# Gated linear attention: scores and query-state products as plain fp32 matmuls instead of three split ones

## The chip, the cores and the metric

The kernel runs on one core of one Trainium2 chip. The metric is the device time of one execution in microseconds (us). The engines are PE (the matrix engine; its weight loads are listed on their own as PEld), DVE (VectorE, elementwise work), ACT (ScalarE, activations and copies), POOL (GpSimd, nearly unused here) and SP (SyncE, which issues the DMAs).

## The reference

One layer of an encoder block on 1024 tokens of width 1024, all in float32: a projection, a gated linear attention that runs in both directions, a windowed attention, gates that merge the two, an output projection and a gated feed-forward part. What matters here is the linear attention (4 heads, keys of 128, values of 256):

```python
def _gla_direction(q, k, v, log_g, include_diag):
    ...
    b = jnp.cumsum(log_g, axis=3)
    b_last = b[:, :, :, -1:, :]
    q_dec = q * jnp.exp(b)
    k_inv = k * jnp.exp(-b)
    k_tail = k * jnp.exp(b_last - b)
    mask = jnp.tril(jnp.ones((c, c), dtype=bool), k=0 if include_diag else -1)
    scores = jnp.where(mask, jnp.einsum("bhncd,bhnmd->bhncm", q_dec, k_inv), 0.0)
    o_intra = jnp.einsum("bhncm,bhnme->bhnce", scores, v)
    chunk_kv = jnp.einsum("bhnmd,bhnme->nbhde", k_tail, v)
    ...
    o_inter = jnp.einsum("bhncd,nbhde->bhnce", q_dec, states)
    return (o_intra + o_inter).reshape(bsz, nh, s, dv)
```

It is called once forward and once on the flipped sequence; the two outputs are added. Two of the products are touched by the change: `scores` (decayed queries with inversely decayed keys) and `o_inter` (decayed queries with the running state).

## The kernel before, in words

Nearly all matrix products are made in "split" form: a float32 operand x is cut into a high part h (a copy rounded to the type fp32r, made by ACT) and a low part l = x - h (made by DVE, also fp32r), and the product is three fp32r matmuls, h·h + h·l + l·h, added up in PSUM. This is `mm3` (line 78); `mm` (line 75) is a single matmul, whose form follows the type of its operands. A few matmuls are plain fp32: the warm-up (line 384) and the sums over squares (lines 417, 421, 1010).

The linear attention is one stage. Head by head, the 1024 tokens are cut into chunks of 128 (c = 0 to 7), two chunks make a pair. Five functions do the work of a chunk:

- `g_gates` (line 481, once a pair): loads queries and keys into `qk`, computes the gates and their running sums (`e`, `cs`), and from them the decayed keys of both directions `en` and the decayed queries. Lines 529 and 530 write the queries over `cs` (forward) and `e` (backward); lines 531 to 538 split keys into `kh`, `kl` and queries into `q2f` (forward) and `q2b` (backward), high part in slot 0, low part in slot 1.
- `g_scores` (line 540): splits the values (`vh`, `vl`), transposes the keys and splits them (`kth`, `ktl`), makes the scores of both directions with `mm3` (lines 558 to 560), merges them through a mask into `sp` and splits that (`sh`, `sl`).
- `g_out` (line 569): the chunk's key-value products, the forward state `pf`, the decayed forward state split into `th`, `tl` (lines 581 to 584), and the output: scores times values, plus queries times state (line 594).
- `g_back` and `g_back_out` (lines 598 and 613): the backward state `kb`, its decayed form split into `thb`, `tlb`, and the product of backward queries with it (line 617).
- `g_turn` (line 633): the transposed output, stored to DRAM.

The order of PE is written out by hand (`manual_schedule`, line 660). Step t of lines 662 to 664 runs what the table `at` holds for it: the gates of a pair first, then the transposes of finished chunks, the backward product, `g_out`, and `g_scores`. Scores of chunk n come two steps after step n, its output three steps after. Between them `fill` inserts a fixed number of dense matmuls (46, then 26, then 24 a step) of projections that other stages need. The order of the other engines is not in the source: a planner places their instructions by readiness and modelled cost, and each engine then runs its list strictly in order. A tile with `bufs=2` is one of two buffers; a new tile waits until every reader of the buffer's last owner is done. `q2f` has two buffers, `q2b` of a pair one to three, `cs` and `e` one.

Of the kernel before, what the change touches and what calls it, by code (L numbers as in the profile page):

```python
# [30 lines left out]
def body(tc, i, out):  # L31
    nc = tc.nc
    with ExitStack() as root:
# [447 lines left out]
        def g_gates(hd, c):  # L481


            pr = Chunk()
            for j in range(2):
                a = gla[hd, c + j] = Chunk()
                a.pr, a.j, a.t = pr, j, slice(j * P, (j + 1) * P)
            s, co = c // 4, (c % 4) * P
            for nme in ("q", "k"):
                need((f"{nme}{hd}", s))  # L490
            qk = gtile("qk", (P, 2, 256))
            nc.sync.dma_start(out=qk[:, 0], in_=scr[f"q{hd}", s][:, co:co + 256])
            nc.sync.dma_start(out=qk[:, 1], in_=scr[f"k{hd}", s][:, co:co + 256])
            if hd == 0:

                r = rstd[:, c * P:(c + 2) * P]
                nc.vector.scalar_tensor_tensor(qk[:, 0], qk[:, 0], 128 ** -0.5, r, op0=ALU.mult, op1=ALU.mult)
                nc.vector.tensor_tensor(qk[:, 1], qk[:, 1], r, op=ALU.mult)
            z = chtile((P, 2, 256))
            for d in range(2):  # L500
                mm(z[:, d], upS[:, d, hd * P:(hd + 1) * P], lrS[:, c * P:(c + 2) * P], True, True)
            e = gtile("e", (P, 2, 2, P), bufs=1)
            ef = e.rearrange("p d j t -> p (d j t)")
            nc.scalar.activation(ef, z.rearrange("p d t -> p (d t)"), AF.Exp, scale=-1.0)

            nc.vector.tensor_scalar(ef, ef, float(np.expm1(8.0)), None, op0=ALU.min)
            nc.scalar.activation(ef, ef, AF.Ln, bias=ones[:, 0:1])

            cs = gtile("cs", (P, 2, 2, P), bufs=1)
            csf = cs.rearrange("p d j t -> p (d j t)")  # L510
            nc.vector.tensor_tensor_scan(csf, mask.rearrange("p c t -> p (c t)"), ef, 0.0, op0=ALU.mult, op1=ALU.add)

            pr.sm = gtile("sm", (P, 2, 2, 2), bufs=16)
            nc.vector.tensor_scalar(pr.sm, cs[:, :, :, 63:128:64], -1.0 / 16, None, op0=ALU.mult)
            nc.vector.tensor_tensor(pr.sm[:, :, :, 1], pr.sm[:, :, :, 1], pr.sm[:, :, :, 0], op=ALU.subtract)

            nc.vector.tensor_tensor(e[:, 0], cs[:, 0], cs[:, 0, :, 63:64].to_broadcast([P, 2, P]), op=ALU.subtract)
            nc.vector.tensor_tensor(e[:, 1, :, 1:P], cs[:, 1, :, 0:P - 1], cs[:, 1, :, 63:64].to_broadcast([P, 2, P - 1]),
                                    op=ALU.subtract)
            nc.vector.tensor_scalar(e[:, 1, :, 0:1], cs[:, 1, :, 63:64], -1.0, None, op0=ALU.mult)  # L520

            x1 = cs.rearrange("p d j t -> p d (j t)")
            x2 = e.rearrange("p d j t -> p d (j t)")
            nc.scalar.activation(csf, ef, AF.Exp, scale=-1.0 / 16)
            nc.scalar.activation(ef, ef, AF.Exp, scale=1.0 / 16)
            pr.en = gtile("en", (P, 2, 256))
            nc.vector.tensor_tensor(pr.en[:, 0], x2[:, 0], qk[:, 1], op=ALU.mult)
            nc.vector.tensor_tensor(pr.en[:, 1], x1[:, 1], qk[:, 1], op=ALU.mult)
            nc.vector.tensor_tensor(x1[:, 0], x1[:, 0], qk[:, 0], op=ALU.mult)
            nc.vector.tensor_tensor(x2[:, 1], x2[:, 1], qk[:, 0], op=ALU.mult)  # L530
            pr.kh = gtile("kh", (P, 2, 256), FR)
            pr.kl = gtile("kl", (P, 2, 256), FR)
            nc.scalar.activation(pr.kh, pr.en, AF.Copy)
            nc.vector.tensor_tensor(pr.kl, pr.en, pr.kh.bitcast(F32), op=ALU.subtract)
            pr.q2 = (gtile("q2f", (P, 2, 256), FR), gtile(f"q2b{c}", (P, 2, 256), FR, bufs=(3, 2, 2, 1)[c // 2]))
            for q2, x in zip(pr.q2, (x1[:, 0], x2[:, 1])):
                nc.scalar.activation(q2[:, 0], x, AF.Copy)
                nc.vector.tensor_tensor(q2[:, 1], x, q2[:, 0].bitcast(F32), op=ALU.subtract)

        def g_scores(hd, c):  # L540

# [14 lines left out]
            nc.vector.tensor_tensor(a.ktl, kt, a.kth.bitcast(F32), op=ALU.subtract)  # L556
            sc = chtile((P, 2, P))
            for d in range(2):
                mm3(sc[:, d], a.pr.kh[:, d, a.t], a.pr.kl[:, d, a.t], a.pr.q2[d][:, 0, a.t], a.pr.q2[d][:, 1, a.t],
                    True, True)  # L560
            sp = gtile("sp", (P, P))
            nc.scalar.copy(sp, sc[:, 0])
            nc.vector.copy_predicated(sp, tri, sc[:, 1])
# [5 lines left out]
        def g_out(hd, c):  # L569
# [6 lines left out]
            if c:  # L576
                pf = gla[hd, c - 1].pf
                dec = gtile("dec", (P, 1))
                p = gla[hd, c - 1]
                nc.scalar.activation(dec, a.pr.sm[:, 0, a.j, 0:1], AF.Exp, bias=p.pr.sm[:, 0, p.j, 1:2])  # L580
                th = gtile("th", dt=FR)
                tl = gtile("tl", dt=FR)
                nc.scalar.activation(th, pf, AF.Copy, scale=dec[:, 0:1])
                nc.vector.scalar_tensor_tensor(tl, pf, dec[:, 0:1], th.bitcast(F32), op0=ALU.mult, op1=ALU.subtract)
                nc.vector.scalar_tensor_tensor(a.pf, pf, dec[:, 0:1], kv[:, 0], op0=ALU.mult, op1=ALU.add)
                a.kb = gtile(f"kb{c}", bufs=2 if c < 5 else 1)
                nc.scalar.copy(a.kb, kv[:, 1])
            else:
                nc.vector.tensor_copy(a.pf, kv[:, 0])
                a.kb = None  # L590
            o = chtile((P, 256))
            mm3(o, a.sh, a.sl, a.vh, a.vl, True, c == 0)
            if c:
                mm3(o, a.pr.q2[0][:, 0, a.t], a.pr.q2[0][:, 1, a.t], th, tl, False, True)
            a.ob = gtile(f"ob{c}", bufs=2 if c < 5 else 1)
            nc.scalar.copy(a.ob, o)

        def g_back(hd, c):

            a = gla[hd, c]  # L600
            if c < NC - 1:
                n = gla[hd, c + 1]
                dec = gtile("decb", (P, 1))
                nc.scalar.activation(dec, a.pr.sm[:, 1, a.j, 1:2], AF.Exp, bias=n.pr.sm[:, 1, n.j, 0:1])
                th = gtile("thb", dt=FR)
                tl = gtile("tlb", dt=FR)
                nc.scalar.activation(th, n.kb, AF.Copy, scale=dec[:, 0:1])
                nc.vector.scalar_tensor_tensor(tl, n.kb, dec[:, 0:1], th.bitcast(F32), op0=ALU.mult, op1=ALU.subtract)
                if c:
                    nc.vector.scalar_tensor_tensor(a.kb, n.kb, dec[:, 0:1], a.kb, op0=ALU.mult, op1=ALU.add)  # L610
                a.thb, a.tlb = th, tl

        def g_back_out(hd, c):
            a = gla[hd, c]
            if c < NC - 1:
                o2 = chtile((P, 256))
                mm3(o2, a.pr.q2[1][:, 0, a.t], a.pr.q2[1][:, 1, a.t], a.thb, a.tlb, True, True)
                nc.vector.tensor_tensor(a.ob, a.ob, o2, op=ALU.add)
            if c:
                g_back(hd, c - 1)  # L620
# [773 lines left out]
```

## Time and profile before

| what | value |
|---|---|
| three runs | 1664.22, 1664.38, 1662.86 us; median 1664.22 |
| the profiled execution's own time | its span, 1661.5 us from the first to the last instruction; no other time of it is recorded |
| granted clock of PE, mean | 1.000 |
| linear attention stage with its filling | about 196 to 545 us of the span |
| windowed attention with its filling | about 545 to 765 us |
| output projections, merge | about 765 to 1035 us |
| feed-forward, two parts | about 1035 to 1448 and 1448 to 1661 us |

A row of the profile's groups reads: line, engine, operation, tiles written and read, shapes, count, then busy us and mean ns of one, then the idle time of the engine just before them and what ended it. L76 is the single matmul inside `mm`, so the tiles tell which product it is; `ch` and `mm` are tiles in PSUM. A row of a timeline reads: start, duration, engine, line, operation, tiles; several like records that follow each other are merged, with their count.

### The profile page before, as it was taken

To read this page: it belongs to the slowest core of one execution; us is meant where nothing else is said; L and a number is where in the kernel's file an instruction comes from. 1 tells how busy PE (TensorE), PEld (TensorE's weight loads), DVE (VectorE), ACT (ScalarE), POOL (GpSimd) and SP (SyncE) were. 2 spreads that over 40 slices of the span, in tenths; PEclk is the share of its full clock that TensorE was granted. 3 is DMA by queue.
4 is the path that set the end of the run, shared out by engine and by line. 5 is a ranking of instruction groups with operands and counts; after the bars stand their busy time and mean duration, and the time that the engine had idled before them with its cause. 6 is when DMAs were issued, how large, how long until landed. Compare 5 with 4: busy or idle time off the path is not lost.

```text
span 1661.5 us, 23685 instructions
## 1 busy us (share of the span) xinstructions
PE 1648.4 (99%) x7792; PEld 1368.2 (82%) x7792; DVE 1259.9 (76%) x2616; ACT 890.7 (54%) x1880; POOL 0.2 (0%) x4
## 2 busy tenths in 40 slices
PE   9999999999999999999999999999999999999999
PEld 7888888888888878887888888888888888888887
DVE  8766766888875898866886578887778877779655
ACT  8522464687877588776644556433333333354442
POOL 0000000000000000000000000000000000000000
PEclk9999999999999999999999999999999999999999
DMA  7444452344435633228866645353234444496433
GB/s 235 144 133 145 153 166 92 110 137 125 133 115 156 203 120 105 91 72 257 254 212 190 177 143 169 108 166 117 93 101 151 165 141 133 159 344 198 148 96 120
DMA packets 157499, 252.41 MB, mean 152 GB/s; under 512 B 18142, under 2 KB 43486, under 8 KB 157376
## 3 DMA queue, kind: packets, MB, share of 16 engines
q1 hardware_dynamic: 157376, 250.90, 48.0%
q8 instruction: 61, 1.00, 0.3%
q14 instruction: 62, 0.51, 0.1%
HBM read 183.46 MB, written 67.37 MB: 151 GB/s over the span
## 4 chain that ended last, share of the span: by engine, by line
PE 87%; DVE 5%; ACT 4%; DMA 3%; issue 1%; SPq 0%; ACTq 0%; DVEq 0%
PE mm L76 33%; PE mm L306 7%; PE mm L308 7%; PE mm L307 7%; PE mm L1207 7%; PE ch L76 7%; PE ch L1207 5%; PE ch L308 3%; PE ch L306 3%; PE ch L307 3%; PE ch L830 1%; DVE wl L72 0%; DMA kvr<-skv 0%; DMA wr<-in_w_fi_dram 0%; PE ch L637 0%
## 5 line engine op out<-in xcount | busy, mean ns | idle before, releaser
L70 ACT ACTIVATE wh<-wr 128x512 fp32r<-128x512 f32 x238 | 148.3, 627 | 103.1 <-PE mm L76 77.7
L72 DVE TENSOR_TENSOR wl<-wr,wh 128x512 fp32r<-128x512 f32 x238 | 162.4, 685 | 42.7 <-ACT wh L70 42.0
L298 ACT ACTIVATE wh<-ws 128x512 fp32r<-128x512 f32 x120 | 75.7, 632 | 176.0 <-PE mm L307 84.7
L76 PE MATMUL mm<-wl,xh 128*128 128x512 f32 x320 | 127.4, 398 | 0.0
L76 PE MATMUL mm<-wh,xh 128*128 128x512 f32 x320 | 126.6, 396 | 0.8 <-DVE xc L376 0.8
L76 PE MATMUL mm<-wh,xl 128*128 128x512 f32 x320 | 126.5, 395 | 0.0
L76 PE MATMUL mm<-xh,wh 128*128 128x512 f32 x256 | 103.0, 403 | 0.2 <-ACT wh L70 0.2
L76 PE MATMUL mm<-xl,wh 128*128 128x512 f32 x256 | 102.1, 399 | 0.1
L299 DVE TENSOR_TENSOR wl<-ws,wh 128x512 fp32r<-128x512 f32 x120 | 82.0, 684 | 22.6 <-ACT wh L298 22.6
L298 ACT ACTIVATE wh<-wr 128x512 fp32r<-128x512 f32 x60 | 37.9, 632 | 105.2 <-issue 49.4
L298 ACT ACTIVATE wh<-a 128x512 fp32r<-128x512 f32 x64 | 40.5, 633 | 90.9 <-PE ch L1207 42.3
L76 PE MATMUL mm<-xh,wl 128*128 128x512 f32 x256 | 88.8, 403 | 0.0
L299 DVE TENSOR_TENSOR wl<-a,wh 128x512 fp32r<-128x512 f32 x64 | 44.2, 690 | 42.8 <-ACT wh L298 42.4
L76 PEld LDWEIGHTS mm<-wh,xh 128*128 128x128 f32 x320 | 60.2, 188 | 11.3 <-DVE xc L376 1.2
L76 PEld LDWEIGHTS mm<-wh,xl 128*128 128x128 f32 x320 | 60.2, 188 | 10.5
L76 PEld LDWEIGHTS mm<-wl,xh 128*128 128x128 f32 x320 | 60.2, 188 | 10.1
L1207 PE MATMUL mm<-hh,wh 128*128 128x512 f32 x176 | 68.5, 389 | 0.0
L1207 PE MATMUL mm<-hl,wh 128*128 128x512 f32 x176 | 68.5, 389 | 0.0
L1207 PE MATMUL mm<-hh,wl 128*128 128x512 f32 x176 | 68.5, 389 | 0.0
L1177 DVE TENSOR_TENSOR hl<-hr,hh 128x512 fp32r<-128x512 f32 x75 | 51.3, 684 | 3.8 <-ACT hh L1176 3.7
L76 PEld LDWEIGHTS mm<-xl,wh 128*128 128x128 f32 x256 | 48.2, 188 | 7.1 <-DVE xl L251 0.7
L76 PEld LDWEIGHTS mm<-xh,wh 128*128 128x128 f32 x256 | 48.2, 188 | 6.9 <-ACT wh L70 0.7
(579 smaller groups left out, 4880.8 us busy)
## 6 DMA issues: line engine op xcount, KB each, us to landing
wr<-in_w_fi_dram SPq DMA_DIRECT2D x102, 256.0 KB, 2.9
wr<-in_w_f_dram SPq DMA_DIRECT2D x80, 256.0 KB, 2.8
wr<-in_w_t_dram SPq DMA_DIRECT2D x80, 256.0 KB, 2.8
B<-c SPq DMA_DIRECT2D x44, 256.0 KB, 2.2
T<-tx SPq DMA_DIRECT2D x44, 256.0 KB, 3.0
a<-in_w_fo_dram SPq DMA_DIRECT2D x44, 256.0 KB, 5.4
hr<-T SPq DMA_DIRECT2D x44, 256.0 KB, 2.7
wr<-in_w_ob_dram SPq DMA_DIRECT2D x32, 256.0 KB, 3.1
```

Of the source, the lines that this page charges most:

```text
L70: nc.scalar.activation(h, raw, AF.Copy)
L72: nc.vector.tensor_tensor(l, raw, h.bitcast(F32), op=ALU.subtract)
L76: nc.tensor.matmul(o, a, b, start=start, stop=stop)
L298: nc.scalar.activation(h, src, AF.Copy)
L299: nc.vector.tensor_tensor(l, src, h.bitcast(F32), op=ALU.subtract)
L306: nc.tensor.matmul(o, h[:, c], x[kk][0], start=start and kk == 0, stop=False, skip_group_check=True)
L307: nc.tensor.matmul(o, h[:, c], x[kk][1], start=False, stop=False, skip_group_check=True)
L308: nc.tensor.matmul(o, l[:, c], x[kk][0], start=False, stop=kk == nk - 1, skip_group_check=True)
L830: nc.tensor.transpose(pt[:, h], a.p[:, h, (kb - a.b0) * P:(kb - a.b0 + 1) * P], ident)
L1177: nc.vector.tensor_tensor(l, r, h.bitcast(F32), op=ALU.subtract)
L1207: nc.tensor.matmul(ys[m], a[:, c], b, start=f0, stop=f1, skip_group_check=True)
```

## The change

Queries, keys and decayed states are no longer split. The decayed queries go straight into `q2f` and `q2b` as float32 (128 x 256 instead of two parts), the scores take `en` and these in one plain fp32 matmul a direction instead of three fp32r ones, and the decayed states `th` and `thb` are single float32 tiles that are multiplied with the queries in one plain fp32 matmul each. `kh`, `kl`, `tl` and `tlb` disappear with the instructions that made them. Values, transposed keys, masked scores, the key-value products and everything outside this stage stay split.

```diff
@@ g_gates
-            nc.vector.tensor_tensor(x1[:, 0], x1[:, 0], qk[:, 0], op=ALU.mult)
-            nc.vector.tensor_tensor(x2[:, 1], x2[:, 1], qk[:, 0], op=ALU.mult)
-            pr.kh = gtile("kh", (P, 2, 256), FR)
-            pr.kl = gtile("kl", (P, 2, 256), FR)
-            nc.scalar.activation(pr.kh, pr.en, AF.Copy)
-            nc.vector.tensor_tensor(pr.kl, pr.en, pr.kh.bitcast(F32), op=ALU.subtract)
-            pr.q2 = (gtile("q2f", (P, 2, 256), FR), gtile(f"q2b{c}", (P, 2, 256), FR, bufs=(3, 2, 2, 1)[c // 2]))
-            for q2, x in zip(pr.q2, (x1[:, 0], x2[:, 1])):
-                nc.scalar.activation(q2[:, 0], x, AF.Copy)
-                nc.vector.tensor_tensor(q2[:, 1], x, q2[:, 0].bitcast(F32), op=ALU.subtract)
+            pr.q2 = (gtile("q2f"), gtile(f"q2b{c}", bufs=(3, 2, 2, 1)[c // 2]))
+            nc.vector.tensor_tensor(pr.q2[0], x1[:, 0], qk[:, 0], op=ALU.mult)
+            nc.vector.tensor_tensor(pr.q2[1], x2[:, 1], qk[:, 0], op=ALU.mult)
@@ g_scores
             for d in range(2):
-                mm3(sc[:, d], a.pr.kh[:, d, a.t], a.pr.kl[:, d, a.t], a.pr.q2[d][:, 0, a.t], a.pr.q2[d][:, 1, a.t],
-                    True, True)
+                mm(sc[:, d], a.pr.en[:, d, a.t], a.pr.q2[d][:, a.t], True, True)
@@ g_out
-                th = gtile("th", dt=FR)
-                tl = gtile("tl", dt=FR)
+                th = gtile("th")
                 nc.scalar.activation(th, pf, AF.Copy, scale=dec[:, 0:1])
-                nc.vector.scalar_tensor_tensor(tl, pf, dec[:, 0:1], th.bitcast(F32), op0=ALU.mult, op1=ALU.subtract)
...
             if c:
-                mm3(o, a.pr.q2[0][:, 0, a.t], a.pr.q2[0][:, 1, a.t], th, tl, False, True)
+                mm(o, a.pr.q2[0][:, a.t], th, False, True)
@@ g_back
-                th = gtile("thb", dt=FR)
-                tl = gtile("tlb", dt=FR)
-                nc.scalar.activation(th, n.kb, AF.Copy, scale=dec[:, 0:1])
-                nc.vector.scalar_tensor_tensor(tl, n.kb, dec[:, 0:1], th.bitcast(F32), op0=ALU.mult, op1=ALU.subtract)
+                a.thb = gtile("thb")
+                nc.scalar.activation(a.thb, n.kb, AF.Copy, scale=dec[:, 0:1])
...
-                a.thb, a.tlb = th, tl
@@ g_back_out
-                mm3(o2, a.pr.q2[1][:, 0, a.t], a.pr.q2[1][:, 1, a.t], a.thb, a.tlb, True, True)
+                mm(o2, a.pr.q2[1][:, a.t], a.thb, True, True)
```

## The prediction

> **What bounds the kernel now.** I read the page first, then the stretch of the program that the change touches, then the waits of PE in it.
>
> ```profile
> span 1661.5 us, 23685 instructions
> PE 1648.4 (99%) x7792; PEld 1368.2 (82%) x7792; DVE 1259.9 (76%) x2616; ACT 890.7 (54%) x1880; POOL 0.2 (0%) x4
> PE 87%; DVE 5%; ACT 4%; DMA 3%; issue 1%; SPq 0%; ACTq 0%; DVEq 0%
> ```
>
> PE is busy 99% of the span and holds 87% of the chain that ended last. The ends of matmuls are modelled, so I do not use their durations; I use the distance from one start to the next, which is what a record costs in an unbroken stream.
>
> ```profile
> 196.00:545.00 349.00, 346.81 (x1897) 295.18 (x1898) 255.88 (x692) 244.78 (x654) 0.00 (x0) 1.00 0.44 133
> ```
>
> This is the table by stretches; the columns are the stretch, its length, then the busy time of PE, weight loads, DVE, ACT and POOL, and the granted clock. It is the linear attention stage with its dense filling. The clock is granted in full (1.00), PE is busy 346.81 of 349.00 us, DVE 255.88 and ACT 244.78. So DVE and ACT work is worth something here only where PE waits for it:
>
> ```profile
> PE ch L76 <- DVE sh L566: 1.1, 3, 0.7
> PE ch L76 <- DVE ktl L556: 0.5, 1, 0.5
> ```
>
> These are the rows of PE's waits (total us, times, longest). Only these two kinds in the stage, 1.6 us together, wait for work of linear attention. The change is therefore first a sum over matmul records, and second the end of four short waits.
>
> **The matmuls that are replaced.** Counts first:
>
> ```profile
> L76 PE MATMUL ch<-q2f,kh 128*128 128x128 f32 x64 | 13.3, 290 | 0.0
> L76 PE MATMUL ch<-q2b,kh 128*128 128x128 f32 x64 | 12.4, 276 | 0.0
> L76 PE MATMUL ch<-th,q2f 128*128 128x256 f32 x56 | 14.5, 281 | 0.0
> L76 PE MATMUL ch<-thb,q2b 128*128 128x256 f32 x56 | 14.5, 281 | 0.1
> ```
>
> In these names the moving operand stands before the stationary one. Each triple uses its high stationary (scores) or its high moving operand (states) twice, so there are 32 + 32 = 64 triples for scores (128 columns move) and 28 + 28 = 56 for products with states (256 columns move). Their rhythm, from the timeline of PE (start, us, engine, line):
>
> ```profile
> 385.57 0.42 PE L76 MATMUL ch<-q2f,kh 128*128 128x128 f32 x2
> 385.83 0.28 PE L76 MATMUL ch<-q2f,kl 128*128 128x128 f32 x1
> 385.94 0.39 PE L76 MATMUL ch<-q2b,kh 128*128 128x128 f32 x2
> 386.16 0.27 PE L76 MATMUL ch<-q2b,kl 128*128 128x128 f32 x1
> 386.27 0.45 PE L76 MATMUL mm<-xh,wh 128*128 128x512 f32 x1
> ```
>
> The six score records of one chunk take 386.27 - 385.57 = 0.70 us, 0.117 each; the first carries about 0.03 from the transposes before it, which stays, and the rest go at 0.112 (385.94 to 386.16 is two records).
>
> ```profile
> 384.15 0.28 PE L76 MATMUL ch<-th,q2f 128*128 128x256 f32 x1
> 384.27 0.28 PE L76 MATMUL ch<-tl,q2f 128*128 128x256 f32 x1
> 384.39 0.28 PE L76 MATMUL ch<-th,q2f 128*128 128x256 f32 x1
> 384.51 0.40 PE L76 MATMUL mm<-xh,wl 128*128 128x512 f32 x1
> ```
>
> A state product takes 384.51 - 384.15 = 0.36 us, 0.119 a record. So a record of 256 columns costs hardly more than one of 128.
>
> **What a plain fp32 matmul costs.** The kernel has a few already: the warm-up of line 384, the sums over squares of line 417 (512 columns) and of line 421 (2 columns).
>
> ```profile
> 4.68 0.94 PE L76 MATMUL ch<-ones 128*128 128x128 f32 x7
> 47.30 1.88 PE L76 MATMUL ch<-acc,ones 128*128 128x512 f32 x4
> 49.01 1.84 PE L76 MATMUL ch<-ones,acc 128*128 128x2 f32 x16
> ```
>
> Line 417 issues two matmuls and leaves four records, line 421 issues eight and leaves sixteen: a plain fp32 matmul is two records. With 512 columns one record takes (49.01 - 47.30) / 4 = 0.428 us. With 2 columns it takes 0.11 (1.84 us for sixteen, the last end modelled), and with 128 columns, at the end of the warm-up, (0.94 - 0.275) / 6 = 0.111, where 0.275 is about the length of one such record. So there is a floor of about 0.112 a record, for 2 columns as for 128, and above it the time grows with the columns. No row shows 256 columns in plain fp32. Without any shape assumed it lies between 0.112 and 0.428. The split matmuls say how it goes between: a 512-column record there costs 0.227,
>
> ```profile
> 1448.31 29.92 PE mm L1207 x132
> ```
>
> (29.92 / 132, from the chain of waits), and a 256-column one 0.119, or 52% of it. Plain fp32 at 256 is then between 0.214 (half of 0.428) and 0.224 (52%); I take 0.214, as at 0.214 the floor of 0.112 is far away.
>
> **The sum.** Scores: per triple three records become two, 3 x 0.112 = 0.336 to 2 x 0.112 = 0.224, 64 times: -7.2 us (with 0.117 a record before, -8.1). State products: 3 x 0.119 = 0.357 to 2 x 0.214 = 0.428, 56 times: +4.0 us (at 0.224: +5.1). PE's stream becomes 3.2 us shorter, between 2.1 and 4.2. PE's order is fixed by hand and the filling counts dense matmuls, not time, so all of this reaches the end of the stage, and from there the end.
>
> The two parts of the change pull against each other: the scores sit on the floor, where a record less is a gain, and the state products stand above it, where plain fp32 streams longer than three split records.
>
> The Trainium skill, "FP8 and Floating Point Precision", section "TensorE Precision Notes", states a rule that speaks against the change: true fp32 takes four passes through the array. The trace agrees as to streaming, since two records at 0.428 are four times half a record; it does not agree as to four loads, since it has two records a matmul. What the sum is if each of four passes pays the floor stands below as a rival.
>
> **What goes from DVE and ACT.**
>
> ```profile
> L534 DVE TENSOR_TENSOR kl<-en,kh 128x512 fp32r<-128x512 f32 x16 | 10.9, 684 | 0.1
> L538 DVE TENSOR_TENSOR q2f<-cs,q2f 128x256 fp32r<-128x256 f32 x16 | 6.7, 417 | 0.0
> L608 DVE SCALAR_TENSOR_TENSOR tlb<-kb,decb,thb 128x256 fp32r<-128x256 f32 x28 | 13.4, 480 | 4.8 <-ACT thb L607 4.4
> L533 ACT ACTIVATE kh<-en 128x512 fp32r<-128x512 f32 x16 | 9.9, 621 | 0.4 <-DVE en L527 0.4
> ```
>
> DVE loses 16 of the first, 16 of the second and as many for q2b, and 28 of the third with 28 like it in line 584: 10.9 + 2 x 6.7 + 2 x 13.4 = 51 us of busy time. ACT loses line 533 and the two copies of line 537. All of it is hidden behind PE's 346.81 us except where PE waited. The longest of those waits, DVE's and PE's timeline together:
>
> ```profile
> 248.84 0.68 DVE L534 TENSOR_TENSOR kl<-en,kh 128x512 fp32r<-128x512 f32 x1
> 249.43 0.41 DVE L538 TENSOR_TENSOR q2f<-cs,q2f 128x256 fp32r<-128x256 f32 x1
> 249.77 0.41 DVE L538 TENSOR_TENSOR q2b<-e,q2b 128x256 fp32r<-128x256 f32 x1
> ...
> 250.43 0.23 DVE L566 CAST sh<-sp 128x128 fp32r<-128x128 f32 x1
> 249.74 0.28 PE L76 MATMUL ch<-vh,ktl 128*128 128x256 f32 x1
> 250.71 0.39 PE L76 MATMUL ch<-vh,sh 128*128 128x256 f32 x1 [0.68 <-DVE sh L566]
> ```
>
> PE needs sh and gets it 0.97 us after the record before, 0.85 more than 0.12. Right in front of sh on DVE stand kl, q2f and q2b, which the change takes out: from 248.84 to about 250.10, 1.26 us, more than PE waited. So this wait ends, and by the same order the other three, which are shorter. From start to start they cost 0.85 / 0.68 times what the page counts, so 1.6 us are about 2.0 us (estimate). I take -2.0; the ends are 0, if something else on the way to sh comes next, such as the copy of the scores by ACT, and -2.0.
>
> The multiplies of lines 529 and 530 stay, 417 ns each, but write into q2f and q2b instead of over cs and e. No DMA is added, removed or moved, and the ACT copies th and thb stay, with another output type, at no change (estimate, from the like copies around).
>
> Together -3.2 - 2.0 = -5.2 us: the span goes from 1661.5 to 1656.3. The median of the runs (1664.22) stands 2.7 above the span of the profiled execution; I take this distance as constant: **1659.0 us**.
>
> One term has no row: DVE's and ACT's order is set anew by the planner when instructions go, here and in the windowed attention behind. In the order of before PE's waits in the stage are 1.6 us, and behind it the largest is
>
> ```profile
> PE ch L76 <- DVE pl L834: 1.5, 1, 1.5
> ```
>
> A new order could lose these or have as many more; I take 0, with about 3 us to each side.
>
> **The rivals.**
>
> *A. Only the matmuls count.* New waits take the place of the old ones, and -3.2 alone is left: 1661.0. For it: the four waits are accidents of one order of DVE, and the next order may have its own. Against it: DVE loses a fifth of its 255.88 us.
>
> *B. Four passes that each pay the floor.* Scores 4 x 0.112 instead of 3 x 0.112, 64 times, +7.2; states 4 x 0.119 instead of 3 x 0.119, 56 times, +6.7; with the waits gone 1664.2 + 13.9 - 2.0 = 1676. Against it: two records for each matmul in the rows above.
>
> *C. The write of q2f blocks DVE.* This is the rival on the other side. q2f has two buffers, and the product of forward states of the odd chunk two pairs back still reads the old one in the very group of steps in which the gates write the new one. Before, copies filled q2f, well after the multiply; now the multiply itself writes it:
>
> ```profile
> 384.15 0.42 DVE L529 TENSOR_TENSOR cs<-cs,qk 128x256 f32<-128x256 f32 x1
> 389.14 0.22 DVE L566 CAST sh<-sp 128x128 fp32r<-128x128 f32 x1
> 390.15 0.28 PE L76 MATMUL ch<-vh,sh 128*128 128x256 f32 x1
> ```
>
> PE reads the old q2f from 384.15 to about 384.67 (the rows of the state product), so the multiply at 384.15 would hold DVE for some 0.5 us, with en, pf, ktl and sh queued behind it. But sh has 390.15 - 389.36 = 0.8 us of slack, and about 0.6 + 0.33 + 0.33 + 0.40 = 1.7 us of DVE work ahead of it (kl, q2f, q2b, tl) goes. The block decides only from 2.5 us on. If the planner put the multiply so early that it held DVE for 3.2 us, 0.7 in each of 14 groups (16 pairs of chunks, less the first two, which find free buffers): 1664.2 - 3.2 + 9.8 = 1671.
>
> *D. More waits end.* All of PE's waits in this stage and the longest behind it: -4.2 from the matmuls, -2.0, -1.5 to -3: about 1656.
>
> **How the numbers follow.** Chances: the forecast 0.58, A 0.22, D 0.10, C 0.06, B 0.04. What one can tell from no change here is about 0.2%, 3.3 us. The forecast and D lie beyond it, A just within (3.2), B and C on the other side: faster 0.68; some of the forecast's own spread and some of A's cross the bound in both directions, which I let cancel; within 0.2% 0.22, slower 0.10. The range reaches from 1654.5 (D with the better end) to 1664.0 (A with the weaker end of the matmuls, 2.1, and a new order that costs 2 us); it leaves out B, C and a little beyond.
>
> **What would show it.** In the changed profile score records come as 128 records of "q2f,en" and "q2b,en" at 0.112 from start to start, state records as 112 with 256 columns at 0.214; rows of kl, kh, tl and tlb are gone; the waits of PE for sh and ktl at 249, 267 and 286 us are gone; the stage ends about 5 us earlier, and everything behind is shifted by as much. Records of 256 columns at 0.25 or more, four records a matmul, or a DVE multiply into q2f that waits long for PE, would prove me wrong.

## The result and the profile after

| kernel | median of the runs | lowest to highest | span of the profiled execution |
|---|---|---|---|
| before | 1664.27 us (4 runs) | 1662.86 to 1664.38 | 1661.5 us |
| after | 1657.02 us (4 runs) | 1656.48 to 1659.58 | 1655.7 us |

The ratio is 0.9951, with a 95% interval of 0.994 to 0.9962: the changed kernel is faster by half a per cent, 7.2 us, and the interval does not reach 1.

The page of the changed kernel, first its span, then the busy times, then the chain that ended last:

```profile
span 1655.7 us, 23275 instructions
PE 1643.6 (99%) x7672; PEld 1362.6 (82%) x7672; DVE 1221.1 (74%) x2512; ACT 873.3 (53%) x1832; POOL 0.2 (0%) x4
PE 90%; DVE 3%; ACT 3%; DMA 2%; issue 1%; SPq 0%; DVEq 0%; ACTq 0%
```

PE has 120 records fewer (7792 to 7672): 64 triples and 56 triples became pairs of records. DVE has lost 38.8 us of busy time and ACT 17.4. PE's share of the last chain went from 87% to 90%, DVE's from 5% to 3%.

The groups of the new matmuls (counts are records):

```profile
L76 PE MATMUL ch<-th,q2f 128*128 128x256 f32 x56 | 16.7, 380 | 0.0
...
L76 PE MATMUL ch<-q2b,en 128*128 128x128 f32 x64 | 12.4, 275 | 0.0
```

The backward state products and the forward scores have rows with the same counts. 28 state products in each direction left 56 records, 32 score matmuls left 64: two records for each plain fp32 matmul, as in the rows of the sums over squares before. Their rhythm, from the timeline of PE in the middle of the stage:

```profile
378.63 0.60 PE L76 MATMUL ch<-th,q2f 128*128 128x256 f32 x2
378.88 0.82 PE L76 MATMUL mm<-xh,wl 128*128 128x512 f32 x2
379.54 0.39 PE L76 MATMUL mm<-xh,wh 128*128 128x512 f32 x1
...
380.22 0.39 PE L76 MATMUL ch<-q2f,en 128*128 128x128 f32 x2
380.44 0.39 PE L76 MATMUL ch<-q2b,en 128*128 128x128 f32 x2
```

There is a trap in such rows. From the start of the state product to the next row are only 0.25 us, which looks like two records of 0.125. But the two 512-column records behind it then take 379.54 - 378.88 = 0.66 us instead of 2 x 0.227 = 0.45. So the start noted for the second record of a plain matmul is not to be taken at its word here: its time shows up behind the next record. Over both rows, 379.54 - 378.63 - 0.45 = 0.46 us go to this state product. So single gaps mislead, and I used sums.

That can be done exactly here. PE's order is written by hand, and the 7432 records that do not belong to the changed products follow each other in the same order in every kernel compared here. Laid side by side, each gap between two starts has a counterpart, and the differences can be summed by what lies in the gap. A gap with a changed product is taken together with the gap behind it, since part of the product's time shows up there. From 190 to 545 us of the kernel before, in us, after minus before:

| what lies in the gap | gaps | difference |
|---|---|---|
| the scores of a chunk | 32 | -7.23 |
| forward state product | 28 | +1.88 |
| backward state product | 28 | +1.84 |
| other records of 256 columns (here PE waited for sh, sl, ktl) | 292 | -3.15 |
| other records of 512 and 128 columns | 1092 | -0.40 |
| the stage | | -7.06 |

The stage by itself, in the table by stretches, and what is left of PE's waits from 190 to 560 us:

```profile
196.00:540.00 344.00, 343.50 (x1786) 291.00 (x1787) 217.14 (x588) 228.10 (x607) 0.00 (x0) 1.00 0.45 137
```

```profile
PE mm L76 <- DVE xc L376: 0.8, 1, 0.8
```

PE was idle 2.19 us of the stage before (349.00 - 346.81) and is idle 0.50 us now. The only wait listed belongs to the entry into the stage and was there before. No wait for sh or ktl is listed any more, though of the last one (287 us before) two gaps of 0.22 us instead of 0.12 remain (283.59 to 284.03). Why they ended can be seen at the place of the longest one, in the timelines of DVE and PE:

```profile
246.75 0.42 DVE L530 TENSOR_TENSOR q2f<-cs,qk 128x256 f32<-128x256 f32 x1
...
247.43 0.42 DVE L531 TENSOR_TENSOR q2b<-e,qk 128x256 f32<-128x256 f32 x1
247.76 0.42 DVE L549 TENSOR_TENSOR ktl<-ch,kth 128x256 fp32r<-128x256 f32 x1
248.09 0.29 DVE L555 COPY_PREDICATED sp<-tri,ch 128x128 f32<-128x128 uint32 x1
248.42 0.23 DVE L558 CAST sh<-sp 128x128 fp32r<-128x128 f32 x1
...
249.54 0.48 DVE L575 SCALAR_TENSOR_TENSOR pf<-pf,dec,ch 128x256 f32<-128x256 f32 x1 [0.57 <-PE ch L76]
249.22 0.28 PE L76 MATMUL ch<-vh,ktl 128*128 128x256 f32 x1
249.34 0.28 PE L76 MATMUL ch<-vh,sh 128*128 128x256 f32 x1
```

sh is done at 248.65 and read at 249.34, 0.69 us to spare, where PE had waited 0.68. Now it is DVE that waits for PE (the 0.57 before pf).

The stage begins at the same distance from the span's start as before (0.1 us later), ends 6.95 us earlier, and the last matmul of the program starts 5.8 us earlier: 1.2 us were given back behind the stage, in gaps of the windowed attention (0.46 at 755 us, 0.2 at 770) and of the later products (0.45 at 1061, 0.16 at 1459). A second profiled execution of the change, below, gives back 1.1 us, at 755 and 770 again but not at 1061. Why these gaps are longer was not followed up.

### The profile page after: what moved, and what is told of

It reads as the page before. It is cut to its first block, busy times and chain, and to the rows that moved or that the text cites. A ratio compares the mean times of both kernels' runs of the same rounds, so it can differ in the third digit from the quotient of the medians.

```text
span 1655.7 us, 23275 instructions
## 1 busy us (share of the span) xinstructions
PE 1643.6 (99%) x7672; PEld 1362.6 (82%) x7672; DVE 1221.1 (74%) x2512; ACT 873.3 (53%) x1832; POOL 0.2 (0%) x4
## 4 chain that ended last, share of the span: by engine, by line
PE 90%; DVE 3%; ACT 3%; DMA 2%; issue 1%; SPq 0%; DVEq 0%; ACTq 0%
PE mm L76 36%; PE ch L76 8%; PE mm L306 7%; PE mm L308 7%; PE mm L307 7%; PE mm L1194 7%; PE ch L1194 5%; PE ch L306 3%; PE ch L307 3%; PE ch L308 3%; PE ch L817 1%; DMA kvr<-skv 1%; DMA lo<-b 0%; PE ch L624 0%; PE ch L545 0%
## 5 line engine op out<-in xcount | busy, mean ns | idle before, releaser
L76 PE MATMUL mm<-wh,xh 128*128 128x512 f32 x320 | 130.8, 409 | 0.8 <-DVE xc L376 0.8
```

What stands on the lines that cost most here:

```text
L76: nc.tensor.matmul(o, a, b, start=start, stop=stop)
```

## The experiments

The theory at the start: PE sets the time. Each score triple that loses a record gains 0.112 us, each state product loses about 0.07, and the work that goes from DVE and ACT is worth the waits it ends and no more. The rivals: the gain comes from DVE and ACT and not from the matmuls; or it comes from a luckier order of the planner. Every ratio below is against the kernel before on the same chip.

The stage as the gaps between PE's starts show it, all against the same profiled execution of before (us):

| kernel | scores | forward states | backward states | other 256-column gaps | the rest | stage |
|---|---|---|---|---|---|---|
| change | -7.23 | +1.88 | +1.84 | -3.15 | -0.40 | -7.06 |
| change again | -7.23 | +1.87 | +1.85 | -3.14 | -0.59 | -7.24 |
| plain scores only | -7.24 | +0.64 | -0.41 | -0.92 | -0.25 | -8.18 |
| plain scores only, again | -7.23 | +0.66 | -0.36 | -0.95 | -0.33 | -8.21 |
| plain states only | +0.10 | +2.04 | +1.82 | -1.43 | -0.30 | +2.23 |
| change, all splits still made | -7.23 | +3.44 | +1.83 | +1.46 | +0.32 | -0.18 |
| change, key and query splits still made | -7.23 | +3.22 | +2.48 | +0.95 | -0.29 | -0.87 |
| change, state splits still made | -7.23 | +1.87 | +1.85 | -2.55 | +0.08 | -5.98 |
| plain scores, low parts of queries on POOL | -7.24 | +1.30 | -0.37 | -0.14 | -0.15 | -6.60 |
| before, low parts on POOL | 0.00 | +0.79 | -0.35 | +10.04 | +3.13 | +13.61 |
| plain scores, late query splits | -7.23 | -0.04 | -0.37 | -1.96 | -0.47 | -10.07 |

### Each half by itself

Plain scores only: keys are not split, queries still are, for the state products, which stay split.

```diff
-            pr.kh = gtile("kh", (P, 2, 256), FR)
-            pr.kl = gtile("kl", (P, 2, 256), FR)
...
+            pr.qs = (gtile("qsf"), gtile("qsb"))
+            nc.vector.tensor_tensor(pr.qs[0], x1[:, 0], qk[:, 0], op=ALU.mult)
+            nc.vector.tensor_tensor(pr.qs[1], x2[:, 1], qk[:, 0], op=ALU.mult)
...
-            for q2, x in zip(pr.q2, (x1[:, 0], x2[:, 1])):
+            for q2, x in zip(pr.q2, pr.qs):
...
+                mm(sc[:, d], a.pr.en[:, d, a.t], a.pr.qs[d][:, a.t], True, True)
```

> Only the scores are plain fp32; the products with states stay split (queries keep a float32 copy beside their two parts, keys are not split). The ledger theory (scores -7.2 us, state products +3.7 to +4, ended waits about -3): the state term is gone, the score term stays, and with kl gone from DVE most of the waits end: -7.2 and -1 to -3, about 1655 us, faster than the changed kernel. The rival (the forms of the matmuls cancel, the gain is the 51 us of DVE work less): only 11 us of DVE work go, so no better than about 1662.

Measured: 1655.92 us against 1665.7, ratio 0.9937 (0.9924 to 0.9949); measured again on another chip:

> The kernel with plain scores and split state products once more, beside the changed kernel. The ledger theory: PE's own records are 3.7 us shorter than in the change (no plain state products), of which the splits that it keeps on DVE give back 2 to 3 as waits: 0 to 3 us faster than the change, ratio to before 0.993 to 0.995. The rival (DVE's relief is what counts): slower than the change, since DVE keeps 40 of the 51 us.

1655.23 us against 1665.22, 0.994 (0.9928 to 0.9953). Beside it, on the same chip, ran the change itself:

> The changed kernel itself, on the same chip and against the same runs of before as the next three. Both theories: the ratio of the first comparison again, 0.994 to 0.996.

1656.14 us, 0.9947 (0.9934 to 0.9959). The scores' gain is the same -7.23 in every kernel that has plain scores. Half the change is at least as good as the whole: the medians are 0.9 us apart and the traces' stages 1.0 us, but the intervals overlap. So the rival that the gain comes from DVE's and ACT's lesser work fails: by it, with only 11 of 51 us of DVE work gone, this kernel should have stayed near 1662 us.

Plain states only: queries and keys are split for the scores as before, the states are not.

```diff
+            pr.kh = gtile("kh", (P, 2, 256), FR)
+            pr.kl = gtile("kl", (P, 2, 256), FR)
...
+            pr.qs = (gtile("qsf", (P, 2, 256), FR), gtile("qsb", (P, 2, 256), FR))
+            for qs, x in zip(pr.qs, pr.q2):
+                nc.scalar.activation(qs[:, 0], x, AF.Copy)
+                nc.vector.tensor_tensor(qs[:, 1], x, qs[:, 0].bitcast(F32), op=ALU.subtract)
...
+                mm3(sc[:, d], a.pr.kh[:, d, a.t], a.pr.kl[:, d, a.t], a.pr.qs[d][:, 0, a.t], a.pr.qs[d][:, 1, a.t],
+                    True, True)
```

> Only the products with states are plain fp32; the scores stay split with kh, kl and both parts of the queries; tl and tlb are gone. The ledger theory: +3.7 to +4.0 from 56 state products, less 0 to 2 us of ended waits: 1666 to 1668 us, slower than before. The rival: 27 us of DVE work less, faster than before, about 1661.

Measured: 1665.49 us, 0.9997 (0.9988 to 1.0006). The state products cost 2.04 + 1.82 = 3.86 us as worked out, and the other 256-column gaps, where waits end, bring 1.4 back. In the runs' times it makes no difference that can be told; the expected 1666 to 1668 us was just missed, and the rival's 1661 clearly.

### The matmuls without the relief

The matmuls of the change, but all the split parts are still made by ACT and DVE and then read by nobody.

```diff
+            pr.kh = gtile("kh", (P, 2, 256), FR)
+            pr.kl = gtile("kl", (P, 2, 256), FR)
...
+                nc.vector.tensor_tensor(qs[:, 1], x, qs[:, 0].bitcast(F32), op=ALU.subtract)
...
+                tl = gtile("tl", dt=FR)
+                nc.vector.scalar_tensor_tensor(tl, pf, dec[:, 0:1], th, op0=ALU.mult, op1=ALU.subtract)
...
+                tl = gtile("tlb", dt=FR)
+                nc.vector.scalar_tensor_tensor(tl, n.kb, dec[:, 0:1], a.thb, op0=ALU.mult, op1=ALU.subtract)
```

> The changed kernel with all its removed splits still made (kh, kl, both parts of the queries, tl, tlb), though nothing reads them: DVE and ACT do the work of before, PE that of the change. The ledger theory: -7.2 + 3.7 from the matmuls; the waits need not return in full, since nothing on PE waits for these tiles and they only stand in front of others in DVE's order: 1658.5 to 1661. The rival: no gain is left, 1664.

Measured: 1664.8 us, 0.9994 (0.9986 to 1.0003). That is a miss for the sum over matmuls: by it the kernel should have kept 3 us or more. The waits of PE from 190 to 560 us in this kernel:

```profile
PE ch L76 <- DVE sh L566: 2.2, 3, 1.1
...
PE ch L76 <- ACT th L582: 0.8, 2, 0.4
```

Two places in the timelines of DVE and PE, that of the longest wait and the next one for sh:

```profile
249.70 0.42 DVE L539 TENSOR_TENSOR qsb<-q2b,qsb 128x256 fp32r<-128x256 f32 x1
...
250.23 0.48 DVE L585 SCALAR_TENSOR_TENSOR pf<-pf,dec,ch 128x256 f32<-128x256 f32 x1
250.62 0.23 DVE L566 CAST sh<-sp 128x128 fp32r<-128x128 f32 x1
249.50 0.28 PE L76 MATMUL ch<-vh,ktl 128*128 128x256 f32 x1
250.90 0.39 PE L76 MATMUL ch<-vh,sh 128*128 128x256 f32 x1 [1.12 <-DVE sh L566]
...
267.15 0.29 DVE L563 COPY_PREDICATED sp<-tri,ch 128x128 f32<-128x128 uint32 x1
267.38 0.69 DVE L72 TENSOR_TENSOR wl<-wr,wh 128x512 fp32r<-128x512 f32 x1
267.99 0.22 DVE L566 CAST sh<-sp 128x128 fp32r<-128x128 f32 x1
```

From the start of PE's last ktl record to the start of the CAST to sh are 1.12 us, where before there were 0.69 (249.74 to 250.43). What is new in between is pf, 0.39 us from start to start, which stood behind sh before. At 267 the planner put wl, a dense matmul's operand, between sp and sh: 0.61 us. DVE's order is another one than before, and here it is a bad one.

By the gaps, the matmuls did what was worked out: -7.23 for the scores, +1.83 for the backward states. The forward states should cost +1.9 and cost +3.44: 0.72 and 0.71 of that are two places where PE now waits for th (at 339 and 476 us of before). The other gaps became 1.8 us longer, where the change made them 3.5 shorter. So with the same matmuls the stage is 6.9 us shorter without the splits (-7.06 against -0.18). About 3.5 of these are the old waits that end; the rest, some 3.4, are waits that this kernel's order made, or made longer, and that the change does not have.

### Which of the splits it is

Kept in turn: only the dead splits of keys and queries (on DVE 24 us that stand in front of sh), and only the dead tl and tlb (27 us on DVE, elsewhere). The theory of position says that the first costs most, the theory of amount that they cost about the same.

> The changed kernel with the dead splits of keys and queries alone (kh, kl and both parts of the queries; no tl, tlb). If what stands in front of sh counts, nearly all of the loss of the kernel with all dead splits is here: 5 to 6 us above the change, ratio 0.998 to 0.999. If the amount counts: 24 of 51 us of DVE work, half the loss, 0.997.

> The changed kernel with the dead low parts of the states alone (tl, tlb). If what stands in front of sh counts: 1 to 2 us above the change, ratio 0.995 to 0.996, since tl stands once a chunk behind th. If the amount counts: 27 of 51 us, half the loss, 0.997.

Measured: with keys and queries 1662.38 us, 0.9983 (0.9974 to 0.9992); with the states 1658.98 us, 0.9962 (0.995 to 0.9975), against 1664.59. The longest kind of wait in the stage, first of the kernel with dead key and query splits, then of that with dead state splits, which has no wait for sh at all:

```profile
PE ch L76 <- DVE sh L566: 1.8, 4, 0.9
```

```profile
PE ch L76 <- DVE ktl L549: 0.2, 1, 0.2
```

About the same busy time of DVE costs 6.2 us of the stage in the one place (-7.06 to -0.87) and 1.1 in the other (-7.06 to -5.98). In the times the first ratio excludes the 0.997 of the theory of amount, by little; the interval of the second includes it, and only its trace speaks for the theory of position. In the first kernel DVE's order around 249 us is nearly that of before again (qsf, ktl, kl, qsb, sp, sh, and pf behind), and PE waits 0.48 us there; around 267 wl stands in front of sh as in the kernel above, and the wait is 0.94. So the splits of keys and queries take the slack in front of sh, and without slack every order has its accidents. Two things are mixed in: keys and queries also keep their copies on ACT, and each kernel has one order of the planner, which was not varied by itself. How much is the work and how much is the order that came with it stays open.

### The price of a column

The disputed cost by itself, in the kernel changed: behind the sums over squares, matmuls of 64 to 512 columns whose results nobody uses, six plain ones and twelve split records for each size.

```diff
+                    for n in (64, 128, 192, 256, 320, 384, 512):
+                        probe = chtile((P, HT))
+                        for _ in range(6):
+                            mm(probe[:, :n], acc[0][:, :P], acc[1][:, :n], True, True)
+                        for _ in range(4):
+                            mm3(probe[:, :n], xh[0][0][:, :P], xl[0][0][:, :P], xh[1][0][:, :n], xl[1][0][:, :n],
+                                True, True)
```

> The changed kernel with a measuring block put in after the sums of line 421: for 64, 128, 192, 256, 320, 384 and 512 moving columns six plain fp32 matmuls and four split triples, back to back, on operands that are there anyway; their results go nowhere. The floor theory (a record costs the greater of about 0.112 us and its streaming time; a plain matmul is two records at 0.835 ns a column, a triple three at 0.417): plain 0.224, 0.224, 0.32, 0.43, 0.53, 0.64, 0.86 us; triple 0.336, 0.336, 0.336, 0.36, 0.42, 0.50, 0.68 us; they cross between 192 and 256 columns, near 205. The rival (four passes that each pay the floor): plain 0.448 at 64 to 256 columns, above the triple everywhere.

The time of the whole (1689.36 us, one run) says nothing but that the block was added. From the timeline of PE, the starts of the blocks and a few split records:

```profile
57.48 2.16 PE L76 MATMUL ch<-acc,acc 128*128 128x192 f32 x12
...
59.57 0.27 PE L76 MATMUL ch<-xl,xh 128*128 128x192 f32 x1
...
60.69 0.27 PE L76 MATMUL ch<-xh,xl 128*128 128x192 f32 x1
60.80 2.78 PE L76 MATMUL ch<-acc,acc 128*128 128x256 f32 x12
...
63.53 0.28 PE L76 MATMUL ch<-xl,xh 128*128 128x256 f32 x1
...
64.60 0.28 PE L76 MATMUL ch<-xl,xh 128*128 128x256 f32 x1
...
64.84 3.40 PE L76 MATMUL ch<-acc,acc 128*128 128x320 f32 x12
```

The granted clock is 1.00 in both stretches used. Split records: 192 columns (60.69 - 59.57) / 10 = 0.112 us, 256 columns (64.60 - 63.53) / 9 = 0.119. Plain records, from block to block less the twelve split ones: 192 columns (60.80 - 57.48 - 12 x 0.112) / 12 = 0.165, 256 columns (64.84 - 60.80 - 12 x 0.119) / 12 = 0.218. So a plain matmul against a triple costs 0.330 against 0.336 at 192 columns and 0.435 against 0.357 at 256: they cross a little above 192 columns (205 had been expected). Scores (128) lie well on the one side, state products (256) on the other.

### Moving the splits, to POOL or to a later place

If the low parts are what is in the way, POOL, which is idle, could make them. First in the kernel with plain scores (the low parts of the queries), then in the kernel before (those of keys and queries):

```diff
-                nc.vector.tensor_tensor(q2[:, 1], x, q2[:, 0].bitcast(F32), op=ALU.subtract)
+                nc.gpsimd.tensor_tensor(q2[:, 1], x, q2[:, 0].bitcast(F32), op=ALU.subtract)
```

> Plain scores, split state products, and the low parts of the queries made on POOL instead of DVE (32 instructions, DVE 13 us less). The ledger theory: the matmuls' -7.2, and the waits that the kernel with plain scores still has (for sh, sl and th, about 2.4 us) mostly end, unless POOL is so slow that a product waits for it: ratio to before 0.992 to 0.9935, the best of all. If POOL is too slow or disturbs DVE, no gain over plain scores alone.

> The kernel before with its matmuls untouched; the low parts of keys and queries are made on POOL instead of DVE (48 instructions, DVE 24 us less). This prices the waits alone. The ledger theory: PE's waits for sh and ktl end, -2 to -3 us, ratio 0.998 to 0.999. The rival (DVE's relief is the whole gain): -4 us or more, 0.9975 or less. If POOL's parts come too late for the scores: slower than before.

Neither reached the gain expected of it. For the first, the case that came had been named, a POOL that is slow or disturbs DVE; for the second another had, POOL's parts coming too late for the scores, and the gaps of the scores are unchanged (0.00). The first took 1657.23 us, 0.995 (0.9937 to 0.9962), and is not better than plain scores with the splits on DVE; the second took 1679.47 us, 1.0083 (1.007 to 1.0097), slower than before. The kernel before with POOL, group of the keys' low parts, then DVE's timeline while POOL was at work (it ran kl from 249.70 to 251.00, q2f to 251.69):

```profile
L534 POOL TENSOR_TENSOR kl<-en,kh 128x512 fp32r<-128x512 f32 x16 | 22.8, 1427 | 285.3 <-ACT kh L533 285.3
```

```profile
250.37 0.31 DVE L563 COPY_PREDICATED sp<-tri,ch 128x128 f32<-128x128 uint32 x1 [0.46 <-ACT sp L562]
250.72 0.37 DVE L566 CAST sh<-sp 128x128 fp32r<-128x128 f32 x1
251.12 0.72 DVE L567 TENSOR_TENSOR sl<-sp,sh 128x128 fp32r<-128x128 f32 x1
```

POOL needs 1427 ns where DVE needed 684, and DVE's own work is slower meanwhile: the CAST to sh took 0.37 us instead of 0.23, sl 0.72 instead of 0.29 (0.29 also in the kernel before at 250.69). The waits in the stage of this kernel:

```profile
PE ch L76 <- DVE sh L566: 3.6, 6, 1.1
PE ch L76 <- ACT kth L555: 2.5, 4, 0.7
PE ch L76 <- DVE sl L567: 1.9, 6, 0.9
```

Now sh is late six times instead of three, sl six times too, and ACT's kth, which PE had not waited for, is late too. DVE, which was spared 24 us of subtractions, lost nearly all of it again: 43 of its instructions took longer by more than 0.12 us than their like that did not meet POOL, 23.7 us in sum. Every one of them ends a fixed time after an instruction of POOL, 0.02 us for 128x2 elements, 0.08 for the CAST, 0.28 for 128x256, as if it had stood still until that one was done. All of them have their inputs in SBUF. The instructions that read a tile in PSUM (ktl, sp, pf) took as long beside POOL as without it (0.42, 0.30 and 0.47 us). The late kth comes of the same: DVE's small instructions L102 to L104, otherwise 0.16 us, take up to 1.26, and in all four places where kth is late ACT has just waited 0.75 to 1.23 us for their result, with kth queued behind:

```profile
338.12 1.26 DVE L102 TENSOR_TENSOR rt<-rt,rl 128x2 f32<-128x2 f32 x1
340.31 0.91 ACT L631 ACTIVATE ob<-ob,ors 128x256 f32<-128x256 f32 x2 [1.23 <-DVE ors L104]
```

The other way out is to leave the splits on DVE and make them later. In the kernel with plain scores, the queries' halves are not needed before the state product, so each is split at the end of `g_scores`:

```diff
-            for q2, x in zip(pr.q2, pr.qs):
-                nc.scalar.activation(q2[:, 0], x, AF.Copy)
-                nc.vector.tensor_tensor(q2[:, 1], x, q2[:, 0].bitcast(F32), op=ALU.subtract)
...
             nc.vector.tensor_tensor(a.sl, sp, a.sh.bitcast(F32), op=ALU.subtract)
+            q2, x = a.pr.q2[c % 2], a.pr.qs[c % 2]
+            nc.scalar.activation(q2[:, 0], x, AF.Copy)
+            nc.vector.tensor_tensor(q2[:, 1], x, q2[:, 0].bitcast(F32), op=ALU.subtract)
```

> Plain scores and split state products as before, but the queries are split later: the forward ones behind the scores of the even chunk, the backward ones behind those of the odd chunk, so that the splits no longer stand in front of sh in the step of the gates. The theory that what counts is the DVE work in front of sh and ktl: the matmuls' -7.2 and the waits as in the change, -2 to -3: the stage 9.5 to 10.5 us shorter, ratio 0.992 to 0.9935, the best of all. The rival (the amount of DVE work counts, wherever it stands): as plain scores with early splits, 0.994.

Measured: 1654.41 us (1653.78 to 1654.51) against 1664.59, 0.9936 (0.9924 to 0.9949). Its stage is 10.07 us shorter, as expected; the ratio is a hair above what was expected. Timelines of DVE and PE:

```profile
248.57 0.41 DVE L563 TENSOR_TENSOR q2f<-qsf,q2f 128x256 fp32r<-128x256 f32 x1
248.90 0.21 DVE L559 CAST sh<-sp 128x128 fp32r<-128x128 f32 x1
249.04 0.41 DVE L563 TENSOR_TENSOR q2b<-qsb,q2b 128x256 fp32r<-128x256 f32 x1
249.17 0.39 PE L76 MATMUL ch<-vh,sh 128*128 128x256 f32 x1
```

sh is in time by 0.06 us, although the planner put the split of q2f in front of it here; only kl and the split of q2b are gone from there. This is the fastest kernel of the study by its median, and by the trace: it has the scores' -7.23, not the states' +3.7, and most of the waits are gone (of the four, the one at 287 us stays, and two gaps in front of sl are 0.20 us longer than before). In the ratios it cannot be told from plain scores with early splits (0.9937 and 0.994), so by the times alone the rival, that the amount of DVE work counts wherever it stands, is not refuted.

## Why the prediction was right, point by point

**What bounds the kernel.** PE, as read. After the change its idle time in the stage is 0.50 us.

**Scores, -7.2.** -7.23 measured, in every kernel with plain scores. The count of 64 triples, two records a plain matmul and the floor of 0.112 all hold. The upper value of -8.1 does not: the 0.117 a record came from the transposes in front, which stay.

**State products, +4.0.** +3.72, of which -0.27 is one gap in front of thb at 455 us that was too long before (0.48 us from start to start, where a 512-column record takes 0.23); without it +3.99. So 0.428 a product, interpolated from 512 columns, was right; the block of columns gives 0.435, and the weaker end of +5.1 was not reached.

**Waits, -2.0.** The four waits named brought 0.84, 0.41, 0.62 and 0.26, in sum 2.13. The term as a whole was mis-sized: gaps without changed products shrank by 3.55 us. Two more, at 373 and 441 us, had stood in the kernel before without being listed as waits:

```profile
373.20 0.28 PE L76 MATMUL ch<-vl,sh 128*128 128x256 f32 x1
373.56 0.39 PE L76 MATMUL ch<-vh,sl 128*128 128x256 f32 x1
```

From 373.20 to 373.56 are 0.36 us where a record takes 0.12, with no wait shown beside it: 0.24 us each time. In the kernels with dead splits they are gone too (0.20 and 0.17 us are left of the 0.36 where all splits are made, 0.12 in the other two), so most of this does not need the lesser work on DVE and comes with the order. Behind five of these six waits the next gap was too long as well, 0.22 us instead of 0.12, which gives another 0.5. Some 0.4 is spread over small gaps. The value of -2.0, given as an end of the range of this term, was therefore no end.

**DVE's 51 us.** The 104 instructions went, as counted, but DVE's busy time fell by 38.8 us. The sum was made of durations that overlap in a dense stretch: a 128x256 subtraction lasts 0.42 us and the next starts 0.33 after it. Nothing in the forecast hung on this number.

**The new order, 0 and 3 to each side.** In the stage no new wait came up. Behind it 1.2 us were lost, in gaps of the windowed attention and the later products, so "all of this reaches the end" holds for 5.8 of 6.95 us. That the span comes out within 0.6 us of the forecast is in part luck: the waits brought 1.55 us more than was put down for them, and the 1.2 lost behind the stage, where the term of the new order had been put at 0, nearly cancel that. The term deserved its range: in the kernel with dead splits, the order that came with the same matmuls cost some 3.4 us and took their whole gain. What the prediction did not say is that the relief and the order hang together. With the work in front of sh gone, the tile comes early enough (0.69 us to spare at 249) that an instruction or two in front of it would not matter; this was not tested with another order.

**From the span to the runs, +2.7.** Wrong by 0.9. Every run of before whose span is on record lies 1.74 to 1.86 us above it; the profiled execution of before, at 1661.5, was one of the quicker ones, with 1663.3 as its time by that distance. Of the 2.0 us between 1659.0 and 1657.02, 0.6 are the span (1655.7 instead of 1656.3), 0.9 this distance, and 0.5 that the profiled execution after (1657.52) lies above its median.

**Rival A, only the matmuls count.** Not here: no new waits took the place of the old ones. In the kernel with all splits still made it is what happened, and more: there new waits took the matmuls' gain as well.

**Rival B, four passes that each pay the floor.** Refuted by the counts (two records each) and by 128-column records at the floor of 0.112. The four passes of the Trainium skill, "FP8 and Floating Point Precision", "TensorE Precision Notes", show in the streaming alone: a split record of 512 columns takes 0.227 us, and if that is one pass, 256 columns stream in about 0.114 (an estimate); the two plain records of 256, 0.436 in sum, are 3.8 times that. Of loads that section says nothing; that four passes would pay four floors was this rival's own addition.

**Rival C, the write of q2f blocks DVE.** The multiply does not wait. Its group, and from DVE's timeline one place where the old q2f had just been read by the forward state product of 378.63:

```profile
L530 DVE TENSOR_TENSOR q2f<-cs,qk 128x256 f32<-128x256 f32 x16 | 6.7, 420 | 0.0
```

```profile
379.71 0.47 DVE L575 SCALAR_TENSOR_TENSOR pf<-pf,dec,ch 128x256 f32<-128x256 f32 x1
380.10 0.42 DVE L530 TENSOR_TENSOR q2f<-cs,qk 128x256 f32<-128x256 f32 x1
```

DVE's idle time before the 16 multiplies is 0.0: the planner put them behind work that takes longer than PE's reading of the old buffer.

**Rival D, more waits end.** Half of it: in the stage they did, behind it the gain was partly lost, and the longest wait there, 1.5 us for pl, is still listed. As a time 1657.02 is nearer to this rival's 1656 than to the forecast's 1659.0, but that comes from the distance between spans and runs; the span of 1655.7 is 0.6 us from the forecast's 1656.3 and about 2 from the rival's best case for it (1661.5 - 7.7 = 1653.8).

**The signs.** 128 score records and 112 state records, no rows of kl, kh, tl, tlb, and the waits at 249, 267 and 286 us gone: all seen. The end of the stage came 6.95 us earlier instead of 5.

## What to carry to other kernels

Price a change of matmul form by records: number of records times the larger of the floor and the streaming time of that form. Here a plain fp32 matmul beats three split ones up to a little above 192 moving columns and loses above, so choose product by product. And before work on other engines is called hidden, look at what is queued in front of the tile that PE fetches last: about the same busy time cost 6.2 us of the stage there and 1.1 elsewhere, though each with one order of the planner. Moving the query splits to a later place on the same engine shortened the stage more than giving them to a slower engine (10.07 against 6.60 us); the intervals of the runs' ratios overlap. A single kernel planned anew can lose a gain of this size to its order, so a part that seems to bring nothing is best looked at gap by gap.

## What the runs showed of the hardware that was not expected

**A floor that does not depend on the form.** Split records of 192 columns take 0.112 us, as long as plain ones of 2 and 128 columns. The Trainium skill, "TensorE: Matmul & The Clock Gate", "LDWEIGHTS (loading the stationary operand)", puts the load of 128 stationary columns at 128 / 1.2 = 107 ns; the floor of 0.112 agrees with a load for each record within 5%, and the profile has as many loads as matmul records (7672 and 7672). The loads' own rows, of 0.19 us, are longer than the distance of two records, so loads overlap, and no run here tells the load from another cause of the floor.

**A clock that halves without a pause.** In the block of columns, the table by stretches (stretch, length, busy PE, weight loads, DVE, ACT, POOL, granted clock, share and GB/s of the DMA):

```profile
49.00:53.00 4.00, 4.00 (x38) 4.00 (x37) 3.26 (x9) 1.44 (x4) 0.00 (x0) 1.00 0.44 151
53.00:56.50 3.50, 3.50 (x19) 3.50 (x18) 3.50 (x8) 2.44 (x4) 0.00 (x0) 0.51 0.00 0
56.50:60.00 3.50, 3.50 (x27) 3.50 (x27) 3.46 (x6) 0.63 (x1) 0.00 (x0) 1.00 0.00 0
```

After 4 us of records of 2 and 64 columns without a gap, the granted clock is 0.51 for 3.5 us, and the 128-column records that fall in it take about twice their time; then it is full again. By the same page's "The HAM clock gate", the clock is halved after an idle window of some 3.4 us. The length agrees, the idleness does not: PE's row is busy 4.00 of 4.00 us. That thin records count as little activity is a guess, from one execution of one kernel.

**POOL holds up DVE.** With POOL at work, a subtraction on DVE with two inputs took 0.72 us instead of 0.29, and it ended 0.15 us after POOL's q2f (251.84 and 251.69); the 43 slowed instructions above all end at such a fixed distance. The Trainium skill's "GPSIMD Engine Reference", "Specifications", names shared SBUF interfaces, with contention for DVE instructions with two SBUF inputs, which agrees with that row. The CAST with one input grew too, from 0.23 to 0.37; the section's other case, DVE instructions in a 2-port mode, would cover it, but no run here shows in which mode it runs.
